# A decoder layer on one core: attention's TensorE work in a written order, projections as counted steps between its parts

## The chip, the cores and the metric

One core of a Trainium2 chip runs the whole kernel. Its engines are TensorE (matrix products, PE in the profile, with its weight loads as PEld), VectorE (DVE), ScalarE (ACT), GpSimd (POOL) and SyncE (SP), which here only issues loads. TensorE reads SBUF and writes PSUM, which has eight banks of 128 x 512 numbers. The metric is device time in microseconds, the median of three runs.

## The reference, cut to what matters

One layer of a hybrid decoder, 512 tokens of width 1024, all in float32. A combined projection of the input gives queries, keys and values of 16 heads of 64, forget gates, the inputs of a state-space branch, and two gates.

```python
q, k, v, f_logit, z, xbc, dt_raw, gate_logit = jnp.split(x @ w_in, ...)
# attention, per head, causal: logit[t, s] = q_t.k_s / 8 + sum of log f between s and t
p = jax.nn.softmax(jnp.where(causal, s, -jnp.inf), axis=-1)
attn = p @ v
gates = sigmoid(gate_logit + b_gates)           # two gates of width 1024
mixed = (gates[0] * (attn @ w_pa) + gates[1] * (ssm @ w_ps)) @ w_out
x = layer_norm(ALPHA * x + mixed)
x = layer_norm(ALPHA * x + (silu(x @ w_fg) * (x @ w_fu)) @ w_fd)
```

## The kernel before

Every float32 operand of a large product is split into a high part (a cast to a shorter format, on ScalarE) and a low part (the difference, on VectorE): `split`, L102 and L103. A product is then three matrix instructions, high by high, high by low and low by high (`mm3`, L144 to L146), which add up in one PSUM bank. There are two kinds of banks, four each: `gps` for projections, `cps` for everything else.

Weights are loaded by SP in chunks of 512 KB (`raw`, four buffers) and split into `whi` and `wlo` (three buffers each, L102 and L103, with priority). A projection is either weight-stationary (`gemm_ws`, 256 output columns into two banks; with the 1024 inputs it is 16 steps of `mm3`, 48 instructions of 512 columns, from two chunks) or input-stationary (`gemm_xs`, 512 output columns into four banks, 32 steps, 96 instructions, four chunks).

The order of the stages is: the state-space branch in four groups, then attention (around L676 of the listing), the second gate `g1` (L690 on), the first gate `g0`, the output projections, the feed-forward part. Each engine works through its queue in order. That order is fixed when the program is built: a scheduler takes instructions by their place in the program text (those under `high_priority` earlier) as their inputs come ready by its own estimate of times. Where a block stands under `manual_schedule`, the engines named in it keep the order of the program text.

Attention works in four groups of four heads. Per group, `att_qk` projects queries and keys (one `gemm_ws` each) and lays them out per head in two tiles: one of 64 rows of the high part with four rows of gate sums under it, which GpSimd fills (L424 memset, L426 and L428 row copies), and one of 128 rows. Their evacuation is a copy on ScalarE (L429), a cast (L430) and a subtraction (L431) on VectorE per head. `att_v` projects the values of two groups at once (`gemm_xs`, L444 and L445). Then `att_head`, for each head:

- scores: for each of four blocks of 128 queries one `cps` bank and two products of 128 to 512 columns (L458, L459);
- softmax per block: mask, negated maximum (L463, VectorE), exponential with row sum (L465, ScalarE), reciprocal (L466) and scaling (L467) on VectorE, in a probability tile `t_y`, of which there are four;
- ten transposes of 128 x 128 into three `cps` banks (L480), each bank split into high and low;
- eight value products into one `cps` bank (L486), of which both halves are added (ScalarE copies one, L490, VectorE adds, L491). Every second head the result is split into `oT`.

The second gate takes a tanh from a `gps` bank into a `t_y` tile (L694) and multiplies `sd`, the state-space result, with it (L695). In the text, projections of a group stand ahead of its heads and the second gate behind all of them; what stands where on TensorE is the scheduler's choice.

Of the kernel before, what the change touches and what calls it, by code (L numbers as in the profile page):

```python
# [2 lines left out]

# [10 lines left out]
ALU = mybir.AluOpType  # L14
# [27 lines left out]
def tile_hybrid_decoder_layer(  # L42
# [62 lines left out]
    def gps():  # L105
        return psum.tile([P, T], F32, name="gps", bufs=4)
# [44 lines left out]
    def gemm_ws(w, c0, nk, rhs, evac, alloc=gps, n=T, chunks=None):  # L151
# [9 lines left out]
        for b in range(2):  # L161
            evac(b, ps[b])

    def gemm_xs(w, c0, lhs, evac, before=None):


        ps = [gps() for _ in range(NT)]
# [11 lines left out]
        if before is None:  # L179
            for kc in range(KD // 2):  # L180
                hi, lo = split_w(fetch(kc), T)
                for tt in range(NT):
                    product(kc, tt, hi, lo)
            return
# [5 lines left out]
        with tc.manual_schedule(engines=ORDERED):  # L190
            for i in range(NT):
# [6 lines left out]
                for tt in range(i + 1):  # L198
                    product(i, tt, *chunks[i])

# [212 lines left out]
    def att_qk(hg, isq, qk):  # L413
        c0 = (C_Q if isq else C_K) + hg * 256
# [19 lines left out]
        gemm_ws(w_in, c0, KD, rhs_x, evac)  # L434

    def att_v(hg):
# [9 lines left out]
        gemm_xs(w_in, C_V + hg * 256, lhs_x, evac)  # L446
        return vt

    def att_head(h, qk, vt, of):
        hh = h % 4  # L450
# [3 lines left out]
        for i in range(NT):  # L454
# [13 lines left out]
            pr.append(pt)  # L468
        ab = big("uh" if h % 2 == 0 else "ul", 4, F32R)
        cc = slot("sq" if h % 2 == 0 else "xw", (P, 2, 256), F32R)  # L470
        pT = {}
        for j, kbs in enumerate(((0,), (1, 3), (2,))):
# [9 lines left out]
            split(hi[:, 0:o], lo[:, 0:o], ps[:, 0:o])  # L482
        po = cps()
# [180 lines left out]
    att_qk(0, True, qk)  # L664
    att_qk(0, False, qk)
# [9 lines left out]
    for hg in range(4):  # L675
        if hg > 0:  # L676
            att_qk(hg, True, qk)
            att_qk(hg, False, qk)
        if hg % 2 == 0:
            vts = att_v(hg)  # L680
        vt = vts[hg % 2]
        for h in range(4 * hg, 4 * hg + 4):
            if h % 2 == 0:
                of = slot("dx")
            att_head(h, qk, vt, of)
            if h % 2 == 1:
                split(oT[h // 2][0], oT[h // 2][1], of)


    for pair in range(4):  # L690
        def evac_g1(b, ps):
            j = 2 * pair + b
# [3 lines left out]
        gemm_ws(w_in, C_G + D + pair * 256, KD, rhs_x, evac_g1)  # L696
# [398 lines left out]
```

## Time and profile before

| | us |
|---|---|
| median of three runs | 1146.16 (1146.07 to 1146.4) |
| the profiled execution's own time | 1149.0 |
| its span, first to last instruction | 1147.3 |
| value projection of heads 0 to 7 | 438.00 to 459.76 |
| first score to last value product | 459.76 to 641.96 |
| rest of the second gate | 641.96 to 661.08 |

A row's start is given in us from the first instruction of the span. The end of a matrix instruction is modelled, and successive ones overlap, so two starts next to each other tell the pace, not the printed duration. Idle time is printed only where nothing at all is under way on the engine by that model.

### The profile page before, as it was taken

Reading aid. Unit: us, or ns where it says so; the run is one execution under the profiler, and the core shown is the slowest. Engines: PE = TensorE matmul, PEld = TensorE weight load, DVE = VectorE, ACT = ScalarE, POOL = GpSimd, SP = SyncE. Lnnn points to the kernel's source line nnn. Section 1 sums busy time; section 2 is a strip of 40 time slices with the busy share of each in tenths; the row PEclk is TensorE's granted clock in tenths of the full one; section 3 lists DMA queues with packets and bytes.
Section 4 is the critical chain, followed back from the end, with each engine's and each line's share of the span. In section 5 each row is a group of like instructions: output and inputs, shape, how many; then the busy total and the mean of one; then the engine's idle time right before and its main releaser. Section 6 shows DMA issues by size and latency. Waiting matters only on the chain.

```text
span 1147.3 us, 15795 instructions
## 1 busy us (share of the span) xinstructions
PE 1118.0 (97%) x6086; PEld 941.3 (82%) x6086; DVE 777.8 (68%) x1223; ACT 527.2 (46%) x912; POOL 134.1 (12%) x165
## 2 busy tenths in 40 slices
PE   7999999999999999999999999999999999999996
PEld 5887778778787788777777888888999999988885
DVE  2679974884786563889598534556997777767326
ACT  2476664454542432666465434214654554453210
POOL 3003130030122100221110000011111111100001
PEclk9999999999999999999999999999999999999998
DMA  6353233233232233211212245381778787465311
GB/s 195 110 169 127 75 112 101 82 111 101 83 94 58 89 92 96 70 57 56 77 53 56 76 127 183 108 204 59 199 184 204 183 195 164 91 231 174 102 55 74
DMA packets 116060, 134.20 MB, mean 117 GB/s; under 512 B 5669, under 2 KB 94481, under 8 KB 115857
## 3 DMA queue, kind: packets, MB, share of 16 engines
q1 hardware_dynamic: 98896, 111.75, 31.8%
q0 software_dynamic: 14640, 14.10, 7.7%
q10 hardware_dynamic: 2448, 7.34, 1.8%
q8 instruction: 48, 0.79, 0.3%
q14 instruction: 28, 0.22, 0.1%
HBM read 128.78 MB, written 4.26 MB: 116 GB/s over the span
## 4 chain that ended last, share of the span: by engine, by line
PE 44%; DVE 3%; issue 3%; DMA 2%; ACT 1%; POOL 0%; POOLq 0%; DVEq 0%; ACTq 0%
PE gps L145 9%; PE gps L144 9%; PE gps L146 9%; PE cps L145 5%; PE cps L146 5%; PE cps L144 4%; DMA rq<-in_w_ffn_up_dram 1%; PE cps L480 1%; PE cps L486 1%; DMA t_sd<-in_x_dram 0%; DVE xr L763 0%; PE cps L458 0%; DMA raw<-in_w_ffn_down_dram 0%; PE cps L459 0%; DVE wlo L103 0%
## 5 line engine op out<-in xcount | busy, mean ns | idle before, releaser
L103 DVE TENSOR_TENSOR wlo<-raw,whi 128x1024 fp32r<-128x1024 f32 x127 | 156.2, 1230 | 189.3 <-ACT whi L102 188.6
L102 ACT CAST whi<-raw 128x1024 fp32r<-128x1024 f32 x127 | 133.4, 1051 | 253.5 <-PE gps L145 101.9
L145 PE MATMUL gps<-xl,whi 128*128 128x512 f32 x456 | 181.2, 397 | 0.0
L144 PE MATMUL gps<-xh,whi 128*128 128x512 f32 x456 | 181.0, 397 | 0.0
L146 PE MATMUL gps<-xh,wlo 128*128 128x512 f32 x456 | 180.8, 396 | 0.0
L102 ACT CAST wh<-rq 128x1024 fp32r<-128x1024 f32 (+1 forms) x84 | 82.2, 980 | 101.7 <-PE cps L145 44.6
L103 DVE TENSOR_TENSOR wl<-rq,wh 128x1024 fp32r<-128x1024 f32 (+1 forms) x84 | 95.0, 1132 | 34.2 <-ACT wh L102 34.1
L144 PEld LDWEIGHTS gps<-xh,whi 128*128 128x128 f32 x456 | 85.9, 188 | 16.3 <-issue 0.2
L145 PEld LDWEIGHTS gps<-xl,whi 128*128 128x128 f32 x456 | 86.0, 189 | 16.1 <-issue 0.2
L146 PEld LDWEIGHTS gps<-xh,wlo 128*128 128x128 f32 x456 | 86.0, 189 | 15.4
L144 PE MATMUL gps<-whi,xh 128*128 128x512 f32 x192 | 76.1, 397 | 1.9 <-ACT whi L102 1.6
L145 PE MATMUL gps<-wlo,xh 128*128 128x512 f32 x192 | 75.8, 395 | 1.0 <-DVE wlo L103 1.0
L146 PE MATMUL gps<-whi,xl 128*128 128x512 f32 x192 | 75.8, 395 | 0.0
L265 DVE SCALAR_TENSOR_TENSOR t_v<-gps,cw,t_v 128x511 f32<-128x511 f32 (+2 forms) x72 | 53.4, 745 | 3.9 <-ACT t_v L262 3.1
L145 PE MATMUL gps<-t_ul,whi 128*128 128x512 f32 x128 | 51.1, 399 | 0.0
L146 PE MATMUL gps<-t_uh,wlo 128*128 128x512 f32 x128 | 51.0, 399 | 0.0
L144 PE MATMUL gps<-t_uh,whi 128*128 128x512 f32 x128 | 50.5, 394 | 0.0
L144 PEld LDWEIGHTS gps<-whi,xh 128*128 128x128 f32 x192 | 36.5, 190 | 10.7 <-ACT whi L102 2.0
L465 ACT ACTIVATE t_y<-t_y,sm 128x128 f32<-128x128 f32 (+1 forms) x64 | 35.7, 559 | 19.4 <-DVE sm L463 17.7
L347 ACT ACTIVATE t_ab<-t_ab,acum 128x128 f32<-128x128 f32 x128 | 41.6, 391 | 5.7 <-DMA t_ab<-ac_d 5.4
L821 POOL DMA_DIRECT2D rq<-in_w_ffn_gate_dram x12 | 15.5, 1294 | 245.7 <-ACT xh L723 159.0
L145 PEld LDWEIGHTS gps<-wlo,xh 128*128 128x128 f32 x192 | 36.5, 190 | 9.3 <-DVE wlo L103 1.9
(567 smaller groups left out, 2761.3 us busy)
## 6 DMA issues: line engine op xcount, KB each, us to landing
raw<-in_w_in_dram SPq DMA_DIRECT2D x80, 512.0 KB, 3.7
rq<-in_w_ffn_gate_dram SPq DMA_DIRECT2D x25, 512.0 KB, 5.8
rq<-in_w_ffn_up_dram SPq DMA_DIRECT2D x25, 512.0 KB, 5.9
raw<-in_w_ffn_down_dram SPq DMA_DIRECT2D x22, 512.0 KB, 4.0
t_ab<-ac_d SPq DMA_DIRECT2D x32, 256.0 KB, 3.3
raw<-in_w_proj_ssm_dram SPq DMA_DIRECT2D x16, 512.0 KB, 3.5
rq<-in_w_ffn_gate_dram POOLq DMA_DIRECT2D x10, 512.0 KB, 7.8
rq<-in_w_ffn_up_dram POOLq DMA_DIRECT2D x10, 512.0 KB, 6.4
```

The source lines that it names most:

```text
L102: nc.scalar.copy(out=hi, in_=src)
L103: nc.vector.tensor_tensor(out=lo, in0=src, in1=hi.bitcast(F32), op=ALU.subtract)
L144: nc.tensor.matmul(out=o, lhsT=l[0], rhs=r[0], start=start, stop=False, skip_group_check=skip)
L145: nc.tensor.matmul(out=o, lhsT=l[0], rhs=r[1], start=False, stop=False, skip_group_check=skip)
L146: nc.tensor.matmul(out=o, lhsT=l[1], rhs=r[0], start=False, stop=stop, skip_group_check=skip)
L265: nc.vector.scalar_tensor_tensor(out=v[:, sh:], in0=ps[:, 0:T - sh], scalar=cw[:, k, blk:blk + 1], in1=v[:, sh:], op0=ALU.mult, op1=ALU.add)
L347: nc.scalar.activation(out=m[:, r, :], in_=m[:, r, :], func=AF.Relu, scale=-1.0, bias=acum[:, c, h:h + 1])
L465: nc.scalar.activation(out=pt[:, 0:n], in_=pt[:, 0:n], func=AF.Exp, scale=-1.0, bias=sm[:, 2:3], accum_out=sm[:, 0:1])
L480: nc.tensor.transpose(out=ps[:, o:o + P], in_=pr[i][:, kb * P:(kb + 1) * P], identity=ident)
L486: nc.tensor.matmul(out=po[:, kb * P:], lhsT=vt[:, kb, hh, :], rhs=pT[kb][j], start=kb == 0 and j == 0, stop=kb == NT - 1 and j == 1)
L821: nc.gpsimd.dma_start(out=self.v(t), in_=self.q(*s_), accum_op=ALU.add)
```

## The change

`gemm_ws` and the plain form of `gemm_xs` become generators (`ws_steps`, `xs_steps`) that issue one step of three products at each call, and evacuate a bank as soon as its last step is issued. `att_head` is cut in three: `att_scores` with the softmax, `att_transposes`, `att_values`. The whole attention part stands under `manual_schedule` for TensorE, so there the text is the order: scores of the next head, a number of steps (`before_t`, 7 if not listed), values of the head before, ten transposes, a number of steps (`after_t`, 3), and so on. The steps come in a chain: queries and keys of group 1, a quarter of the second gate, queries and keys of group 2 (80 steps, heads 0 to 7), then values of groups 2 and 3, queries and keys of group 3, the rest of the second gate (112 steps). On the other engines, scores with softmax, and transposes with their splits, stand under `high_priority`. The second gate's tanh is written into its own bank, not into a `t_y` tile.

```diff
-        for b in range(2):
-            evac(b, ps[b])
+                    if half == nk // 4 - 1 and k == 3:
+                        evac(b, ps[b])
+                    yield
...
+    def xs_steps(w, c0, lhs, evac):
+        ps = [gps() for _ in range(NT)]
+        for kc in range(KD // 2):
+            hi, lo = load_w(w[kc * 256:(kc + 1) * 256, c0:c0 + T], 2, T)
+            for tt in range(NT):
+                for k in range(2):
+                    kt = kc * 2 + k
+                    mm3(ps[tt], lhs(kt, tt), (hi[k], lo[k]), kt == 0, kt == KD - 1)
+                    if kt == KD - 1:
+                        evac(tt, ps[tt])
+                    yield
...
-    for hg in range(4):
-        if hg > 0:
-            att_qk(hg, True, qk)
-            att_qk(hg, False, qk)
-        if hg % 2 == 0:
-            vts = att_v(hg)
-        vt = vts[hg % 2]
-        for h in range(4 * hg, 4 * hg + 4):
...
-            att_head(h, qk, vt, of)
...
-            th = slot("y")
-            nc.scalar.activation(out=th, in_=ps, func=AF.Tanh, scale=0.5, bias=vec[:, 32 + j:33 + j])
-            nc.vector.scalar_tensor_tensor(out=sd[j], in0=th, scalar=1.0, in1=sd[j], op0=ALU.add, op1=ALU.mult)
+                nc.scalar.activation(out=ps, in_=ps, func=AF.Tanh, scale=0.5, bias=vec[:, 32 + j:33 + j])
+                nc.vector.scalar_tensor_tensor(out=sd[j], in0=ps, scalar=1.0, in1=sd[j], op0=ALU.add, op1=ALU.mult)
+            yield from ws_steps(w_in, C_G + D + pair * 256, KD, rhs_x, evac_g1)
+    with tc.manual_schedule(engines={mybir.EngineType.PE}):
+        vts, steps = att_v(0)
...
+        def finish(h, pT):
...
+            att_values(h, pT, vts[(h // 4) % 2], of[0])
...
+        pr, pT = att_scores(0, qk), None
+        gates = gates1()
+        steps = chain(*(att_qk(1, isq, qk) for isq in (True, False)), islice(gates, 16), *(att_qk(2, isq, qk) for isq in (True, False)))
+        before_t = {8: 10, 9: 12, 10: 10, 11: 14, 12: 6, 13: 6, 14: 6}
+        after_t = {8: 4, 9: 4, 10: 4, 11: 8, 12: 3, 13: 4, 14: 3}
+        for h in range(AH):
+            fill(before_t.get(h, 7))
+            if pT is not None:
+                finish(h - 1, pT)
+            with tc.high_priority():
+                pT = att_transposes(h, pr)
+            fill(after_t.get(h, 3))
+            if h == 7:
+                finish(h, pT)
+                pT = None
+                vts, steps = att_v(2)
+                steps = chain(steps, *(att_qk(3, isq, qk) for isq in (True, False)), gates)
+                fill(8)
+            if h < AH - 1:
+                with tc.high_priority():
+                    pr = att_scores(h + 1, qk)
+        finish(AH - 1, pT)
```

How the order on the engines moves is shown at two places. The first is TensorE in the first heads. Before, from the third group of transposes of head 0 (`cps<-ident,t_y`) to its first value products (`cps<-t_uh,t_xtok`); `gps<-xh,whi` and its like are products of a projection:

```order
L480 MATMUL cps<-ident,t_y 128x128 x3
L145 MATMUL gps<-xl_98,whi 128x512
L146 MATMUL gps<-xh_96,wlo 128x512
L144 MATMUL gps<-xh_96,whi 128x512
L145 MATMUL gps<-xl_98,whi 128x512
L480 MATMUL cps<-ident,t_y 128x128 x4
L146 MATMUL gps<-xh_96,wlo 128x512
L144 MATMUL gps<-xh_96,whi 128x512
L486 MATMUL cps<-t_uh,t_xtok 128x512
L145 MATMUL gps<-xl_98,whi 128x512
L146 MATMUL gps<-xh_96,wlo 128x512
L486 MATMUL cps<-t_uh,t_xtok 128x512
```

Now, from the last step ahead of head 0's value products to the first step behind head 1's transposes (the lines count differently in the changed file: L145 to L147 are `mm3`, L499 the transposes, L509 the value products):

```order
L145 MATMUL gps<-xh_96,whi 128x512
L146 MATMUL gps<-xl_98,whi 128x512
L147 MATMUL gps<-xh_96,wlo 128x512
L509 MATMUL cps<-t_uh,t_xtok 128x512 x2
L509 MATMUL cps<-t_uh,t_xtok 128x384 x2
L509 MATMUL cps<-t_sq,t_xtok 128x256 x2
L509 MATMUL cps<-t_uh,t_xtok 128x128 x2
L499 MATMUL cps<-ident,t_y 128x128 x10
L145 MATMUL gps<-xh_96,whi 128x512
L146 MATMUL gps<-xl_98,whi 128x512
L147 MATMUL gps<-xh_96,wlo 128x512
```

Transposes came in groups of one to four, and value products one by one, with products of a projection between them; now eight value products and ten transposes stand in one piece.

The second place is VectorE between the softmax of one head and the next. Before, from the last scaled tile of head 2 (`t_y<-t_y,sm`) over the splits of its transposes (`t_uh`, `t_sq`) and the first masked scores of head 3 (`t_y,sm<-cps,mneg`) to the sum of head 2's values (`t_dx<-cps,t_yo`):

```order
L467 TENSOR_SCALAR t_y<-t_y,sm 128x512
L431 SCALAR_TENSOR_TENSOR t_cbm<-gps,t_btok 64x512
L103 TENSOR_TENSOR t_uh<-cps,t_uh 128x512 x2
L103 TENSOR_TENSOR t_sq<-cps,t_sq 128x256
L463 ISA t_y,sm<-cps,mneg 128x128
L463 ISA sm 128x1
L463 ISA t_y,sm<-cps,mneg 128x256
L463 ISA sm 128x1
L466 RECIPROCAL sm<-sm 128x1
L463 ISA t_y,sm<-cps,mneg 128x384
L463 ISA sm 128x1
L491 TENSOR_TENSOR t_dx<-cps,t_yo 64x512
```

Now, from the last scaled tile of head 2 over the sum of head 1's values and the splits of head 2's transposes to the masked scores of head 3 (L479 masks, L483 scales, L514 sums, L104 splits, `wlo` is a weight chunk's low part):

```order
L483 TENSOR_SCALAR t_y<-t_y,sm 128x512
L104 TENSOR_TENSOR wlo<-raw,whi 128x1024
L514 TENSOR_TENSOR t_dx<-cps,t_yo 64x512
L104 TENSOR_TENSOR t_uh<-cps,t_uh 128x512 x2
L104 TENSOR_TENSOR t_sq<-cps,t_sq 128x256
L104 TENSOR_TENSOR t_hn<-t_dx,t_hn 128x512
L448 CAST t_th<-t_v 64x512
L479 ISA t_y,sm<-cps,mneg 128x128
L479 ISA sm 128x1
L479 ISA t_y,sm<-cps,mneg 128x256
```

The sum of a head's values stood among the masked scores of the next head; now the sum of the head before, and the splits, come behind the softmax and a weight split, and ahead of the next head's masked scores.

## Rows read from the trace of the kernel before

**Rows 1.** Page, busy time of each engine: us (share of the span) xinstructions

```profile
PE 1118.0 (97%) x6086; PEld 941.3 (82%) x6086; DVE 777.8 (68%) x1223; ACT 527.2 (46%) x912; POOL 134.1 (12%) x165
```

**Rows 2.** Windows: from:to us, busy (xcount) PE PEld DVE ACT POOL, clock, DMA

```profile
438.00:459.76 21.76, 21.76 (x98) 18.02 (x96) 7.44 (x10) 6.03 (x10) 0.00 (x0) 1.00 0.32 94
459.76:641.96 182.20, 180.79 (x910) 140.47 (x908) 151.31 (x410) 113.09 (x258) 24.83 (x48) 1.00 0.22 61
641.96:661.08 19.12, 19.12 (x87) 15.82 (x86) 7.04 (x8) 6.36 (x9) 0.00 (x0) 1.00 0.34 100
```

**Rows 3.** Timeline of PE: start, us, engine line op out<-in xcount [idle<-releaser]

```profile
438.00 0.39 PE L144 MATMUL gps<-whi,xh 128*128 128x512 f32 x1
...
459.76 0.22 PE L458 MATMUL cps<-t_v,t_btok 68*128 68x128 f32 x1
...
461.05 0.40 PE L144 MATMUL gps<-xh,whi 128*128 128x512 f32 x1
...
661.08 0.39 PE L144 MATMUL gps<-xh,whi 128*128 128x512 f32 x1
```

**Rows 4.** Groups of PE, 459.76 to 641.9: xcount | busy us, mean ns

```profile
L144 PE MATMUL gps<-xh,whi 128*128 128x512 f32 x132 | 53.7, 407 | 0.0
...
L144 PE MATMUL gps<-whi,xh 128*128 128x512 f32 x32 | 12.6, 394 | 0.0
```

**Rows 5.** Timeline of PE: four transposes, one product, and the next product's start

```profile
475.28 0.60 PE L480 MATMUL cps<-ident,t_y 128*128 128x128 f32 x4
...
475.95 0.40 PE L145 MATMUL gps<-xl,whi 128*128 128x512 f32 x1
```

**Rows 6.** Timeline of PE: value products of 256 and 128 columns in head 1

```profile
477.87 0.28 PE L486 MATMUL cps<-t_xw,t_xtok 128*128 128x256 f32 x1
477.99 0.22 PE L459 MATMUL cps<-t_th,t_cbm 128*128 128x128 f32 x1
...
478.22 0.33 PE L486 MATMUL cps<-t_ul,t_xtok 128*128 128x128 f32 x2
478.39 0.33 PE L458 MATMUL cps<-t_v,t_btok 68*128 68x256 f32 x1
```

**Rows 7.** Waits, 459.76 to 641.9: who waited for whom: us, times, longest us

```profile
PEld cps L480 <- DVE t_y L467: 11.4, 37, 0.8
...
PEld cps L458 <- DVE sm L463: 2.3, 5, 0.6
```

**Rows 8.** Timeline of PE: a score behind a product

```profile
470.20 0.40 PE L144 MATMUL gps<-xh,whi 128*128 128x512 f32 x1
470.81 0.50 PE L458 MATMUL cps<-t_bT,t_xst 68*128 68x512 f32 x1 [0.22 <-DVE sm L463]
```

**Rows 9.** Timeline of DVE: the last probability tile of head 0

```profile
465.86 0.49 DVE L467 TENSOR_SCALAR t_y<-t_y,sm 128x512 f32<-128x512 f32 x1
```

**Rows 10.** Timelines of ACT, then DVE: transposes' splits, values' copy and sum

```profile
475.59 1.07 ACT L102 CAST t_ul<-cps 128x512 fp32r<-128x512 f32 x2 [0.55 <-PE cps L480]
...
478.64 0.58 ACT L490 COPY t_yo<-cps 64x512 f32<-64x512 f32 x1 [1.08 <-PE cps L486]
...
476.24 1.29 DVE L103 TENSOR_TENSOR t_ul<-cps,t_ul 128x512 fp32r<-128x512 f32 x2
...
479.60 0.68 DVE L491 TENSOR_TENSOR t_dx<-cps,t_yo 64x512 f32<-64x512 f32 x1
```

**Rows 11.** Groups of DVE, 459.76 to 641.9: the fill's own work

```profile
L103 DVE TENSOR_TENSOR wlo<-raw,whi 128x1024 fp32r<-128x1024 f32 x21 | 25.7, 1224 | 12.9 <-ACT whi L102 12.7
...
L445 DVE TENSOR_TENSOR t_xtok<-gps,t_xtok 128x256 fp32r<-128x256 f32 x11 | 4.5, 421 | 1.8 <-ACT t_xtok L444 1.8
...
L431 DVE SCALAR_TENSOR_TENSOR t_xdt<-gps,t_xst 64x512 fp32r<-64x512 f32 x6 | 4.2, 695 | 0.1
...
L695 DVE SCALAR_TENSOR_TENSOR t_sd<-t_y,t_sd 128x512 f32<-128x512 f32 x4 | 2.6, 683 | 0.0
...
L430 DVE CAST t_th<-t_v 64x512 fp32r<-64x512 f32 x6 | 2.6, 427 | 0.2
```

More of the change, by code (lines that the diff above doesn't have):

```diff
@@ L2 @@
 from contextlib import ExitStack
+from itertools import chain, islice
 import concourse.bass as bass
@@ L160, in gemm_ws @@
                     mm3(ps[b], (hi[k][:, bs], lo[k][:, bs]), rhs(kt), kt == 0, kt == nk - 1)
-        for b in range(2):
-            evac(b, ps[b])
+                    if half == nk // 4 - 1 and k == 3:
+                        evac(b, ps[b])
+                    yield
     def gemm_xs(w, c0, lhs, evac, before=None):
-        ps = [gps() for _ in range(NT)]
+        ps = [] if before is None else [gps() for _ in range(NT)]
         def fetch(kc):
@@ L179, in gemm_xs @@
         if before is None:
[L180 to L183, printed above, removed]
+            for _ in xs_steps(w, c0, lhs, evac):
+                pass
             return
@@ L482, in att_head, with att_values @@
             split(hi[:, 0:o], lo[:, 0:o], ps[:, 0:o])
+        return pT
+    def att_values(h, pT, vt, of):
+        hh = h % 4
         po = cps()
@@ L663, in tile_hybrid_decoder_layer @@
                 group_x(g + 1, st, pair)
-    att_qk(0, True, qk)
-    att_qk(0, False, qk)
+    for isq in (True, False):
+        for _ in att_qk(0, isq, qk):
+            pass
     group_proj(NG - 1, u)
@@ L674, in tile_hybrid_decoder_layer, with gates1, evac_g1 @@
     oT = [(oslots[2 * i], oslots[2 * i + 1]) for i in range(KD)]
[L675 to L682 removed]
+    def gates1():
+        for pair in range(4):
+            def evac_g1(b, ps, pair=pair):
+                j = 2 * pair + b
+                nc.scalar.activation(out=ps, in_=ps, func=AF.Tanh, scale=0.5, bias=vec[:, 32 + j:33 + j])
+                nc.vector.scalar_tensor_tensor(out=sd[j], in0=ps, scalar=1.0, in1=sd[j], op0=ALU.add, op1=ALU.mult)
+            yield from ws_steps(w_in, C_G + D + pair * 256, KD, rhs_x, evac_g1)
@@ L683, in tile_hybrid_decoder_layer, with fill @@
+    with tc.manual_schedule(engines={mybir.EngineType.PE}):
+        vts, steps = att_v(0)
+        for _ in steps:
+            pass
+        of = {}
+        def finish(h, pT):
             if h % 2 == 0:
-                of = slot("dx")
-            att_head(h, qk, vt, of)
+                of[0] = slot("dx")
+            att_values(h, pT, vts[(h // 4) % 2], of[0])
             if h % 2 == 1:
[L687 to L692, printed above, removed]
-            th = slot("y")
-            nc.scalar.activation(out=th, in_=ps, func=AF.Tanh, scale=0.5, bias=vec[:, 32 + j:33 + j])
-            nc.vector.scalar_tensor_tensor(out=sd[j], in0=th, scalar=1.0, in1=sd[j], op0=ALU.add, op1=ALU.mult)
-        gemm_ws(w_in, C_G + D + pair * 256, KD, rhs_x, evac_g1)
+                split(oT[h // 2][0], oT[h // 2][1], of[0])
+        def fill(n):
+            for _ in range(n):
+                if next(steps, 0) == 0:
+                    break
+        pr, pT = att_scores(0, qk), None
[20 more added lines that the diff above has]
+        finish(AH - 1, pT)
+        for _ in steps:
+            pass
```

15 lines of the change are left out of this document (9 added, 6 removed).

## The prediction

> **What bounds the kernel now.** The page's first view comes first: TensorE is busy for 97% of the span [rows 1], so the kernel can only get shorter where TensorE gets its products out faster. The busy share does not say where that is. The view by windows splits the part that the change touches into three stretches [rows 2]: the value projection ahead of head 0 (438.00 to 459.76 us), the 16 attention heads (459.76 to 641.96), and the rest of the second gate's projections (641.96 to 661.08). TensorE shows as busy in all three (99% in the middle), at a granted clock of 1.00. VectorE is at 34%, 83% and 37%.
>
> The timeline gives the pace. The value projection is 96 products of 512 columns, from the first at 438.00 to the first score at 459.76 [rows 3]: 21.76 / 96 = 0.2267 us a product. The middle stretch has 3 x 132 + 3 x 32 = 492 such products [rows 4], and the tail 576 - 492 = 84 (19.12 / 84 = 0.228, full pace again). Three prices for attention's own work, each read where the instructions stand together:
> - scores of one head, 8 products: 459.76 to 461.05, 1.29 us [rows 3];
> - transposes: four of them and one 512-column product take 475.28 to 475.95, so (0.67 - 0.23) / 4 = 0.11 each, 1.11 for ten [rows 5];
> - value products, 8 a head: two of 512 columns at 0.227, two of 384 at 0.17 (between the 512 and the 256), two of 256 at 0.12 and the last two together 0.17 [rows 6], 1.20 in all.
>
> A head costs 3.60, sixteen 57.6. So the middle stretch would take 492 x 0.2267 + 57.6 = 169.1 at those prices, and it takes 182.2: 13.1 us are lost there, inside time that the profile calls busy. The list of waits shows how: the weight loads wait 11.4 us in 37 places for a scaled probability tile ahead of a transpose, and 2.3 us in 5 places for a score's bank [rows 7]. In the timeline one blocked score stands 0.61 us behind the product before it, of which only 0.22 are printed as idle [rows 8].
>
> Here a rule and the first view disagree. By TensorE's busy time the middle stretch has 182.20 - 180.79 = 1.4 us to give [rows 2]. The Trainium skill (Perfetto Trace Analysis, Identifying the Most-Contended Engine) calls matmul busy time a poor measure, since the instructions are pipelined, and looks at the share of weight loads instead. This trace sides with it: weight loads are busy 83% at full pace and 77% among the heads [rows 2]. Scaled by that ratio the stretch would lose about 13 us, as an estimate. The sum below uses the starts alone.
>
> **The change part by part.** (1) The order. Before, a transpose, a value product or a score stands between two products of a projection wherever the scheduler put it, and TensorE stops there if its input is late. Now each head is: scores, 7 steps of a projection (a step is 3 products, 0.68 us), the value products of the head before, ten transposes, 3 steps, the next scores. No product is added or removed: 576 of 512 columns and 16 heads stand in both, from the first score to the first product of the next gate. Before, that takes 661.08 - 459.76 = 201.3 us [rows 3]. Without a single wait it would now take 576 x 0.2267 + 57.6 = 188.2. The ceiling of the gain is 13.1.
>
> (2) What is late next. I follow one steady head from the start of its scores, at 0. Scores end at 1.29, the 7 steps at 6.05, the value products at 7.25, the transposes at 8.36, the 3 steps at 10.4. The transposes need all four probability tiles. In head 0 of before, with a weight split and a value tile of the projection queued among them on VectorE, the last tile is scaled at 465.86 + 0.49 = 466.35 [rows 9], 6.6 after the first score; so in a steady head they are there with 0.7 or more to spare. Only in head 0, which has no value products in front, does the fourth transpose come early: 461.05 + 21 x 0.2267 + 0.33 = 466.14, a wait of about 0.3, with the restart 0.4.
> The tight place is the next scores at 10.4, each of which needs one of four score banks. These are freed by the value product's copy and sum (0.58 on ScalarE, 0.68 on VectorE) and by the three splits of the transposes (two copies in 1.07, two subtractions in 1.29, a third of half the width) [rows 10]. The value products end at 7.25, their sum at about 7.25 + 0.25 + 0.58 + 0.68 = 8.8, and the subtractions follow at 9.4, 10.0 and 10.4, while the four scores start at 10.4, 10.6, 10.9 and 11.2. It fits with 0.4 to 0.8 to spare if VectorE has nothing else queued ahead.
>
> (3) VectorE's share. Its work does not change: 151.3 + 7.0 us in the two stretches [rows 2], 84% of 188.2. It is only placed otherwise. Per projection of queries or keys the fill costs VectorE two weight splits, four casts and four subtractions, 2 x 1.22 + 4 x 0.41 + 4 x 0.69 = 6.9; per pair of gate columns 2 x 1.22 + 2 x 0.68 = 3.8 [rows 11]. The first 80 steps, spread over heads 0 to 7, are four of the former and one of the latter, 31.4 in all. The groups of fill in the middle stretch add to 25.7 + 4.5 + 16.6 + 2.6 + 9.9 = 59.3 (the third and the last are four groups each, of which one stands in the rows). A head's own work lies then between (151.3 - 59.3) / 16 = 5.75, and (182.2 - 59.3) / 16 = 7.7 if VectorE had no idle at all there. Heads 0 to 7 thus need 77 to 93 us of VectorE and 80 x 0.68 + 8 x 3.60 = 83.2 of TensorE. I take the low end, since it is the measured busy time, and the upper one takes all idle for work. Heads 8 to 15 have 112 steps: 105.0 of TensorE, and of VectorE 33.4 for the fill and 46 to 62 for the heads, always less. The one crowded head is head 3, where nine casts and subtractions and two weight splits fall together, 14 us of full durations; VectorE has caught up by head 4, whose own queue holds one weight split and one subtraction.
>
> (4) The gate's tanh now stays in its bank, and the sum reads it there. That frees the four probability buffers for heads alone, and holds a projection bank for one VectorE instruction longer. No row shows a tanh written to a bank; by the nearest, the same instruction into SBUF and the subtractions that read a bank (0.68 to 0.69 [rows 11]), it is from -0.3 to +0.3 us for each of 8. All eight lie beside TensorE's work, with two free banks: 0 on the path; if that cover were gone, 2.4. (5) The evacuation of a projection's first half is written earlier, which moves nothing that TensorE waits for; outside this part the order on the engines is as before. (6) SP's queue keeps its order of loads, and POOL's its memsets and row copies.
>
> Costs left over: 0.4 in head 0, and at the seams of 16 heads (three changes between kinds of products, a bank that is just late) between 0 and 0.6 a head. The low end is a seam as at 461.05, which costs 0.01 to 0.02, the high end is the blocked score of before. I take 0.15, near the low end, as the bank has 0.4 to spare: 2.4. So 13.1 - 0.4 - 2.4 = 10.3, and I forecast 10: the profiled span goes from 1147.3 to 1137.3, its execution from 1149.0 to 1139.0, and the median of the runs, which lies 2.8 under that execution, from 1146.16 to 1136.2.
>
> **The rivals.**
> - VectorE paces heads 0 to 7. For it: it is 83% busy in the middle stretch, and head 3 has 14 us of it against 10.4 of TensorE. Against: that 83% comes with the same work. At the upper bound it costs 92.8 - 83.2 = 9.6: 188.2 + 9.6 = 197.8, and the median is 1142.7; halfway 1138 to 1140.
> - The scores wait for their banks in every head, and the kernel gets slower. TensorE can no longer run a projection past a late score, and only 2 us of fill stand between the transposes and the scores. For it: before already has scores that wait for a bank [rows 7, 8], and in the order a weight split (1.22) stands on VectorE ahead of the value sum and the splits. If that split starts late, sum and splits end up to 1.2 later, and the scores wait up to 0.8. From 13.1 / 16 = 0.82 a head on, the gain is eaten. With the split and a half-evacuated projection (1.1 more) ahead, it is 1.9 - 0.8 = about 1 a head more: 1147 to 1150. Against: the weight split is released long before the value products end, so VectorE is through with it by then. The Trainium skill (Perfetto Trace Analysis, Optimization Strategy) reads the same gap coming back as a sign of too few buffers for the next tile; four banks for four scores, three transposes and one sum are that case, and the printed waits of before agree in kind.
> - Nothing moves. TensorE is as full as it can be, as its busy row says, and the gaps between starts are the price of changing between kinds of products. Then at most 1.4 come back, 1144.8 to 1146.2. For it: a lone transpose among products costs more than 0.11. Against: the 13.7 us for which the weight loads wait [rows 7] have names of late tiles.
>
> **How the numbers follow.** The forecast, TensorE at its pace with small seams, has 0.70 and lies between 1133.2 (no wait at all) and 1139.5. VectorE as the pace has 0.16 (1138 to 1143), nothing moves 0.08, the banks 0.06. A difference of 0.2% (2.3 us) is about what a measurement of this kernel tells from none: faster 0.86, same 0.08, slower 0.06. The range for 8 in 10 is 1133.0 to 1143.0.
>
> **What would show it.** In the profile after: from the first score to the first product of the next gate 189 to 194 us, where 201.3 were; heads 1, 2, 4 and 5 at 10.4 to 10.7 from score to score; the weight loads' wait for scaled tiles under 2 us; VectorE's busy time over the stretch as before, near 158. The forecast is wrong if that stretch is over 195: with waits of transposes for scaled tiles in heads 2 to 7 it is VectorE, with waits of scores for the splits of the transposes it is the banks. If the stretch is shorter by 10 and the span is not, the time was given back in the next gate or the FFN, which I hold for unlikely, since TensorE bounds those too.

## The result, and the profile after

The changed kernel takes 1137.33 us (median of four runs, 1135.88 to 1138.17) against 1146.28 of the kernel before: a ratio of 0.9914, 95% interval 0.9902 to 0.9926. Run again beside other runs of the kernel before, it took 1137.15 (0.9918, 0.9904 to 0.9933). The forecast was 1136.2 in a range of 1133.0 to 1143.0.

The view by windows, as in [rows 2]: the value projection ahead of head 0, then what is called the stage from here on, from the first score to the first product of the next gate (the last two rows of [rows 2] together).

```profile
438.72:460.48 21.76, 21.76 (x98) 18.02 (x97) 7.43 (x10) 6.03 (x10) 0.00 (x0) 1.00 0.33 94
460.48:651.85 191.37, 190.83 (x994) 163.16 (x992) 157.20 (x417) 118.83 (x266) 25.04 (x48) 1.00 0.24 68
```

The value projection takes the same 21.76. The stage takes 191.37 instead of 201.32 [rows 3], so 9.95 of the gain is there. VectorE does the same work in it, 157.2 against 151.3 + 7.0. The share of weight loads, by which the prediction judged the loss, went from (140.47 + 15.82) / 201.32 = 78% to 85%. It shows the direction and not the size: it is now above the 83% of the value projection while 3.2 us are still lost, and about as many weight loads (992, before 994) show as 163.2 us where they showed as 156.3. That the prediction's scaling by 83% came to the same 13 us was luck. The page's PE row barely moved, from 97% to 98%:

```profile
PE 1108.9 (98%) x6086; PEld 947.4 (83%) x6086; DVE 777.3 (68%) x1223; ACT 526.4 (46%) x912; POOL 134.2 (12%) x165
```

The list of waits of the weight loads in the stage, which answers to [rows 7]:

```profile
PEld cps L509 <- DVE t_xtok L463: 0.5, 1, 0.5
PEld cps L474 <- DVE t_ul L104: 0.5, 2, 0.3
PEld cps L499 <- DVE t_y L483: 0.3, 1, 0.3
...
```

(The two rows left out, 0.3 us each, have no releaser.) Transposes waited 11.4 us in 37 places for a scaled tile; now it is 0.3 in one. Two rows of the list of before, which the prediction passes over, are gone as well: value products that wait for the splits of the transposes. With the two rows of the subtractions (1.1 and 1.0) they come to 7.1 us.

```profile
PEld cps L486 <- ACT t_uh L102: 2.5, 8, 0.3
PEld cps L486 <- ACT t_ul L102: 2.5, 7, 0.6
```

A weight load that waits can still overlap the product before it, so these times are not a sum of what TensorE lost: with the 13.7 us that the prediction names they make 20.8, where the starts give 13.1. The timeline of TensorE in the changed kernel, at the end of head 1, shows a whole pass without a wait (L145 to L147 are the projections, L474 and L475 the scores, L499 the transposes, L509 the value products):

```profile
476.08 0.96 PE L509 MATMUL cps<-t_uh,t_xtok 128*128 128x512 f32 x4
...
477.29 1.28 PE L499 MATMUL cps<-ident,t_y 128*128 128x128 f32 x10
478.32 0.48 PE L145 MATMUL gps<-xh,whi 128*128 128x512 f32 x1
478.64 0.40 PE L146 MATMUL gps<-xl,whi 128*128 128x512 f32 x1
...
480.50 0.23 PE L474 MATMUL cps<-t_v,t_btok 68*128 68x128 f32 x1
...
481.79 0.40 PE L145 MATMUL gps<-xh,whi 128*128 128x512 f32 x1
```

Value products take 1.21 (1.20 foreseen), scores 1.29 (1.29), ten transposes and the product behind them 1.35 (1.11 + 0.23 = 1.34 foreseen). From first score to first score the heads take, by the starts in the timeline:

| head | 0 | 1 | 2 | 3 | 4 | 5 | 6 | 9 | 10 |
|---|---|---|---|---|---|---|---|---|---|
| us | 9.55 | 10.48 | 10.47 | 10.47 | 11.09 | 10.47 | 10.47 | 15.17 | 13.20 |
| at full pace | 9.20 | 10.40 | 10.40 | 10.40 | 10.40 | 10.40 | 10.40 | 14.48 | 13.12 |

(Head 0 has no value products; heads 9 and 10 have 16 and 14 steps. Of the heads not shown, 7 and 13 are 0.3 over full pace.) An undisturbed head is 0.07 to 0.08 over. The three that stand out are head 0, whose fourth transpose waits for its tile, head 4, whose scores wait for their banks (t_ul is a split that frees one), and head 9, whose value products wait for VectorE to finish the value projection's last tile. The waits above have these three names. For head 9, TensorE's row and then the one of VectorE for which it waits:

```profile
573.03 0.40 PE L509 MATMUL cps<-t_sq,t_xtok 128*128 128x256 f32 x2
573.77 0.44 PE L509 MATMUL cps<-t_uh,t_xtok 128*128 128x128 f32 x2 [0.34 <-DVE t_xtok L463]
```

```profile
572.15 1.23 DVE L104 TENSOR_TENSOR wlo<-raw,whi 128x1024 fp32r<-128x1024 f32 x1 [0.76 <-ACT whi L103]
573.30 0.42 DVE L463 TENSOR_TENSOR t_xtok<-gps,t_xtok 128x256 fp32r<-128x256 f32 x1
```

A weight split of 1.23 us stands ahead of the last part of the value tile, which is done at 573.72.

### The profile page after: what moved, and what is told of

The parts are those of the page before. It is cut to its first block, busy times and chain, and to the rows that moved or that the text cites. A ratio compares the mean times of both kernels' runs of the same rounds, so it can differ in the third digit from the quotient of the medians.

```text
span 1136.5 us, 15815 instructions
## 1 busy us (share of the span) xinstructions
PE 1108.9 (98%) x6086; PEld 947.4 (83%) x6086; DVE 777.3 (68%) x1223; ACT 526.4 (46%) x912; POOL 134.2 (12%) x165
## 4 chain that ended last, share of the span: by engine, by line
PE 81%; DVE 9%; issue 4%; POOL 2%; DMA 2%; ACT 2%; POOLq 0%; DVEq 0%; ACTq 0%
PE gps L147 19%; PE gps L146 19%; PE gps L145 19%; PE cps L146 5%; PE cps L147 5%; PE cps L145 5%; PE cps L509 2%; DVE wlo L104 1%; PE cps L499 1%; PE cps L370 1%; DMA rq<-in_w_ffn_up_dram 1%; ACT whi L103 1%; PE cps L474 1%; PE cps L475 1%; PE cps L328 1%
## 5 line engine op out<-in xcount | busy, mean ns | idle before, releaser
L104 DVE TENSOR_TENSOR wlo<-raw,whi 128x1024 fp32r<-128x1024 f32 x127 | 156.2, 1230 | 177.5 <-ACT whi L103 176.5
L145 PE MATMUL gps<-xh,whi 128*128 128x512 f32 x456 | 180.8, 396 | 0.0
L147 PE MATMUL gps<-xh,wlo 128*128 128x512 f32 x456 | 179.6, 394 | 0.0
L104 DVE TENSOR_TENSOR wl<-rq,wh 128x1024 fp32r<-128x1024 f32 (+1 forms) x84 | 94.8, 1130 | 33.2 <-ACT wh L103 33.1
L145 PEld LDWEIGHTS gps<-xh,whi 128*128 128x128 f32 x456 | 86.0, 189 | 17.4 <-issue 0.2
L147 PEld LDWEIGHTS gps<-xh,wlo 128*128 128x128 f32 x456 | 85.9, 188 | 17.5
L145 PE MATMUL gps<-whi,xh 128*128 128x512 f32 x192 | 76.3, 397 | 1.9 <-ACT whi L103 1.6
L147 PE MATMUL gps<-whi,xl 128*128 128x512 f32 x192 | 75.5, 393 | 0.0
L147 PE MATMUL gps<-t_uh,wlo 128*128 128x512 f32 x128 | 51.0, 399 | 0.0
L145 PE MATMUL gps<-t_uh,whi 128*128 128x512 f32 x128 | 50.5, 395 | 0.0
L145 PEld LDWEIGHTS gps<-whi,xh 128*128 128x128 f32 x192 | 36.4, 190 | 10.4 <-ACT whi L103 2.0
L147 PEld LDWEIGHTS gps<-whi,xl 128*128 128x128 f32 x192 | 36.4, 190 | 8.6 <-DVE xl L104 1.1
```

What stands on the lines that cost most here:

```text
L104: nc.vector.tensor_tensor(out=lo, in0=src, in1=hi.bitcast(F32), op=ALU.subtract)
L145: nc.tensor.matmul(out=o, lhsT=l[0], rhs=r[0], start=start, stop=False, skip_group_check=skip)
L147: nc.tensor.matmul(out=o, lhsT=l[1], rhs=r[0], start=False, stop=stop, skip_group_check=skip)
```

## The experiments

Three theories were to be told apart. A: TensorE's order of before put transposes, scores and value products where their inputs were late, and the written order gives the gain. B: the priority on the other engines gives it. C: the time was the price of changing between kinds of products. All runs and what came of them; "stage" is as above, read from the starts in each profile, and each ratio is to the kernel before, run beside it.

| kernel | median us | ratio to before, 95% interval | stage us |
|---|---|---|---|
| before | 1146.28 | 1 | 201.32 |
| after | 1137.33 | 0.9914, 0.9902 to 0.9926 | 191.37 |
| old_order_priority | 1155.68 | 1.0084, 1.0069 to 1.0099 | 210.58 |
| old_order_control | 1162.68 | 1.0134, 1.0114 to 1.0154 | 216.86 |
| no_priority | 1142.35 | 0.9967, 0.9956 to 0.9977 | 196.06 |
| mixed_transposes | 1141.00 | 0.9950, 0.9935 to 0.9965 | 194.68 |
| old_spread_of_fill | 1140.81 | 0.9952, 0.9938 to 0.9967 | 195.57 |
| transposes_2us_earlier | 1141.53 | 0.9948, 0.9931 to 0.9964 | 195.61 |
| scores_1.4us_earlier | 1143.30 | 0.9963, 0.9952 to 0.9975 | 197.3 |
| tanh_in_a_tile | 1135.31 | 0.9898, 0.9883 to 0.9912 | 191.08 |
| after_again | 1137.15 | 0.9918, 0.9904 to 0.9933 | 191.39 |
| gaps_closed | 1135.89 | 0.9905, 0.9888 to 0.9921 | 190.64 |
| gaps_closed_tanh_in_a_tile | 1136.58 | 0.9915, 0.9899 to 0.9930 | 190.39 |

### The old order, with priority and without

The attention part was written so that TensorE goes through the same kinds and shapes of products in the same order as in the kernel before, by a list of counts (S a score, P a projection product, T a transpose, V a value product; code shortened).

```diff
+ORDER = "S8 P12 T P T2 P3 T3 P4 T4 P2 V P2 V2 S V2 S V3 S4 P S2 P6 T P T2 P4 T3 ..."
...
+        for kind, n in ORDER:
+            for _ in range(n):
+                next(work[kind])     # S, and T with its splits, under high_priority
```

> TensorE keeps, product for product, the order of the kernel before (transposes, value products and scores strewn among the projections), but the scores' chain and the transposes with their splits have priority on the other engines, as after, and the tanh stays in its bank. All work is done. Stage from the first score to the first product of the next gate: 201.3 us before, 191.4 after. Theory A (TensorE's written order gives the gain, since the order of before puts products where their inputs are late): 198 to 202, time 1143 to 1147. Theory B (the priority on VectorE and ScalarE gives it, and TensorE's order is nearly free): 191 to 194, time 1137 to 1140. Theory C (the loss of before is the price of changing between kinds of products): unchanged, 201, time 1146; A and C are told apart by mixed_transposes.

Measured: 210.58 and 1155.68, so slower than before, where no theory had put it. So the priority, with the old order of TensorE, does not give the gain that B said. A's number missed too, and the trace says why. The timelines of VectorE in head 1, first of before (L463 negated maximum, L467 scaling), then of this kernel (L500, L504):

```profile
472.36 0.55 DVE L467 TENSOR_SCALAR t_y<-t_y,sm 128x128 f32<-128x128 f32 x2
472.81 0.68 DVE L463 CUSTOM_DVE_ANT_0 t_y<-cps,mneg 128x512 f32<-128x512 f32 x1
...
474.65 0.48 DVE L467 TENSOR_SCALAR t_y<-t_y,sm 128x512 f32<-128x512 f32 x1
```

```profile
471.72 0.69 DVE L500 CUSTOM_DVE_ANT_0 t_y<-cps,mneg 128x512 f32<-128x512 f32 x1
...
473.13 0.26 DVE L504 TENSOR_SCALAR t_y<-t_y,sm 128x128 f32<-128x128 f32 x1
...
473.38 1.06 DVE L504 TENSOR_SCALAR t_y<-t_y,sm 128x256 f32<-128x256 f32 x3
```

With priority, the last tile is ready earlier (474.44 against 475.13) and the first later (473.39 against 472.6), as all four maxima now run ahead of the first scaling. But the old order wants the first tile first. TensorE, before and in this kernel (here L526 is a transpose, L164 a product of the projection):

```profile
472.76 0.27 PE L480 MATMUL cps<-ident,t_y 128*128 128x128 f32 x1
```

```profile
473.45 0.33 PE L526 MATMUL cps<-ident,t_y 128*128 128x128 f32 x1 [0.38 <-DVE t_y L504]
473.53 0.48 PE L164 MATMUL gps<-xl,whi 128*128 128x512 f32 x1
```

The products behind the late transpose come in their order, so most heads keep what their first transpose loses. Measured from each head's first score, the first transposes of the sixteen heads come later than before by 9.1 us in all; the stage is 9.3 longer. (Head by head it is rougher: heads 3 and 11 get theirs back, and behind head 7 a projection waits 1.4 us for its bank.) The Trainium skill (PSUM — Partial Sum Buffer, Engine vs sequencer instructions) says that products on TensorE start in program order, though a weight load may go ahead; the rows agree, since the projection product waits with the transpose.

The same kernel without the priorities was the control.

```diff
-                    with tc.high_priority():
-                        next(work[kind])
+                    next(work[kind])
```

> The kernel of old_order_priority without the priorities: TensorE in the order of the kernel before, the other engines ordered by the scheduler. That one took 210.6 us in the stage and 1155.7 us, 9 over before, with its first probability tile of a head 0.5 to 1 us later and its last 0.6 to 1.3 earlier than before. If the priority is what made it slower (it reorders VectorE for tiles that TensorE's order does not want first): back to 200 to 203, time 1145 to 1148. If the fixed order of TensorE as such, or the other way of writing the code, cost it: 208 to 211, time 1153 to 1156.

Measured: 216.86 and 1162.68, slower still, and both expectations missed. Part of the 216.86 is the clock: in the profiled execution a stretch at a lower granted clock (0.60 in the row below, the column ahead of the last two) falls into head 11, which takes 16.29 us where head 3, whose order on TensorE is the same, takes 15.04 (in before the two take 11.81 and 11.82). In no other profile does one fall into the stage.

```profile
606.00:608.00 2.00, 2.00 (x9) 1.52 (x8) 0.00 (x0) 0.25 (x1) 0.00 (x0) 0.60 0.82 252
```

Less these 1.25, the stage is about 215.6. So the priority was not the harm; it is worth about 5 us of the stage here, and the kernel before does about 14 better with the same order on TensorE. Between them the order on the other engines differs, the tanh's place, and the point at which the second value tiles are taken. This kernel's largest wait in the stage (L525 is a transpose):

```profile
PEld cps L525 <- DVE t_y L504: 18.8, 33, 3.0
...
```

In before it was 11.4 with at most 0.8 at once [rows 7]. In head 3 the trace shows what VectorE's order does. Its second tile is scaled at 491.27 in before, 3.8 us after the head's first score, and here at 494.95, 6.7 us after it, behind a cast and a subtraction of the fill, the last negated maximum and a weight split; TensorE stands for it. The rows of VectorE in before and here, and the one of TensorE here:

```profile
491.27 0.34 DVE L467 TENSOR_SCALAR t_y<-t_y,sm 128x256 f32<-128x256 f32 x1
```

```profile
494.95 0.67 DVE L504 TENSOR_SCALAR t_y<-t_y,sm 128x256 f32<-128x256 f32 x2
```

```profile
495.35 0.44 PE L525 MATMUL cps<-ident,t_y 128*128 128x128 f32 x2 [2.52 <-DVE t_y L504]
```

So the old order of TensorE takes from 201 to about 216 us, as VectorE's order fits it or not; that the scheduler had made both together in the kernel before is the likely reason for its fit, and stays an argument.

### The written order without priority

```diff
-                with tc.high_priority():
-                    pr = att_scores(h + 1, qk)
+                pr = att_scores(h + 1, qk)
```

(The transposes likewise.)

> After without the two priorities; TensorE's order is that of after, word for word. Theory A: casts and subtractions of the fill then stand on VectorE ahead of probabilities and splits, by up to 1 to 3 us, of which heads 1, 2 and 5 have 2 to 3 to spare and heads 3, 4 and 7 nothing: stage 193 to 197 instead of 191.4, time 1139 to 1143. Theory B: the stage goes back to about 201, time 1146 to 1147. Theory C: unchanged, 191.4, time 1137.

Measured: 196.06 and 1142.35, within A. Nearly all of the 4.7 comes from few heads, above all head 3 (12.96 instead of 10.47):

```profile
497.98 0.84 PE L499 MATMUL cps<-ident,t_y 128*128 128x128 f32 x3
500.79 0.98 PE L499 MATMUL cps<-ident,t_y 128*128 128x128 f32 x7 [1.96 <-DVE t_y L483]
```

```profile
498.47 0.42 DVE L448 CAST t_th<-t_v 64x512 fp32r<-64x512 f32 x1
498.90 0.68 DVE L449 SCALAR_TENSOR_TENSOR t_th<-gps,t_v 64x512 fp32r<-64x512 f32 x1
...
499.65 0.68 DVE L514 TENSOR_TENSOR t_dx<-cps,t_yo 64x512 f32<-64x512 f32 x1
500.26 0.47 DVE L483 TENSOR_SCALAR t_y<-t_y,sm 128x512 f32<-128x512 f32 x1
```

A cast and a subtraction of the fill, and a value sum, stand ahead of the scaling for which TensorE waits. So with the written order the priority is worth 4.7 and with the old one about 5; the written order is worth 19.5 without the priority and 19.2 with it, against the old order written by hand, and 5.3 and 10.0 against the kernel before.

### Lone transposes among products

```diff
+                    if not (kb == 2 and i == NT - 1):
+                        between()                       # one product of a projection
...
-            fill(before_t.get(h, 7))
+            fill(before_t.get(h, 7) - (0 if h == 9 else 2))
```

> After, but each head's ten transposes alternate with nine single products of the projection (two steps of the fill ahead of them and one behind are used for that), so that TensorE changes between kinds 350 to 370 times in the stage, where before changes 259 times and after about 80. All work is done. Theory C, the 13.1 us lost before being the price of such changes (0.07 us each): stage 208 to 213 instead of 191.4, time 1154 to 1159. Theories A and B: a lone transpose with its input ready costs no more than one among others; only heads 0, 3 and 4, whose last probabilities come 6.6, 7.4 and 7.6 us after the first score, wait 0.5 to 0.9 each: stage 191 to 195, time 1137 to 1141.

Measured: 194.68 and 1141.00, within A and far from C. In head 2, where the tiles are early:

```profile
487.25 0.27 PE L506 MATMUL cps<-ident,t_y 128*128 128x128 f32 x1
487.27 0.48 PE L151 MATMUL gps<-xl,whi 128*128 128x512 f32 x1
487.59 0.27 PE L506 MATMUL cps<-ident,t_y 128*128 128x128 f32 x1
...
490.01 0.27 PE L506 MATMUL cps<-ident,t_y 128*128 128x128 f32 x1
```

Eight pairs of a transpose and a product take 490.01 - 487.25 = 2.76, 0.345 a pair; less 0.2267 that is 0.118 for a lone transpose, beside 0.11 in a block. Head 2 takes 10.54 instead of 10.47. Changing between transposes and products costs next to nothing, and C falls; lone value products and scores were not tried by themselves. The rest of the 3.3 is transposes that wait for tiles (L506) and scores that wait for a bank (L480 in this kernel), in heads 0, 1, 5 and 7, where heads 0, 3 and 4 were expected:

```profile
PEld cps L480 <- DVE t_sq L104: 1.8, 3, 0.7
PEld cps L506 <- DVE t_y L489: 1.4, 3, 1.0
```

### The fill spread as before

```diff
-        before_t = {8: 10, 9: 12, 10: 10, 11: 14, 12: 6, 13: 6, 14: 6}
+        before_t = {12: 7, 13: 7, 14: 7, 15: 7}
...
-            fill(before_t.get(h, 7))
+            fill(before_t.get(h, 5))
...
-                fill(8)
+                fill(32)
```

> TensorE in a written order with the priorities, but the projections are spread as before: 8 steps a head in heads 0 to 6 and 8 to 11 (5 ahead of the value products, 3 behind the transposes), the value projection of 32 steps in one piece behind head 7, the gate's in heads 12 to 15 and behind. All work is done. A head with 8 steps is 8 x 0.68 + 3.6 = 9.0 us of TensorE, and VectorE has 5.75 to 7.7 of its own work in it and 3.5 of fill. If the spread matters (VectorE paces such heads, and is idle in the 32 steps): 0.3 to 1.2 us a head in 11 or 12 heads, stage 195 to 203, time 1141 to 1149. If it doesn't: 191 to 193, time 1137 to 1139.

Measured: 195.57 and 1140.81, at the low end of the first case (the time 0.2 under it). Waits for scaled tiles are nearly the only ones:

```profile
PEld cps L499 <- DVE t_y L483: 6.0, 11, 1.1
```

With 8 steps, the fourth transpose stands 6.3 us behind the first score, and the last tiles come at 6.2 to 6.9 in most heads, so they take 9.3 to 9.9 us instead of 9.04. Over heads 2 to 5 (476.87 to 514.81) VectorE is busy 36.42 of 37.94 us, 96%. This is the rival of the prediction in which VectorE paces the heads; it comes at 8 steps a head, and the 10 steps of the change avoid it.

### Transposes earlier, scores earlier

```diff
-            fill(before_t.get(h, 7))
+            fill(before_t.get(h, 7) - (0 if h == 9 else 3))
...
-            fill(after_t.get(h, 3))
+            fill(after_t.get(h, 3) + (0 if h == 9 else 3))
```

> After with three steps of the fill moved from ahead of the value products to behind the transposes in every head but head 9: the transposes come 2.04 us earlier, the fourth at 5.6 instead of 7.6 us after the first score. By the times at which after has the last probability tile (6.6, 7.4, 7.6 and 6.4 us in heads 0, 3, 4 and 7, at most 5.7 in the others), the theory of late tiles gives waits of 2.2, 1.8, 2.0 and 0.8 us and 0 to 0.2 elsewhere, less 0.4 that head 0 waits already and 0.6 of the score banks of head 4: stage 195 to 199 instead of 191.4, time 1141 to 1145. If the place of the transposes does not matter: 191, time 1137.

Measured: 195.61 and 1141.53, within the expectation, but spread otherwise: heads 0 and 7 lose 2.0 and 1.8, head 3 loses 1.3, and head 4, for which 2.0 less 0.6 was expected, gains 0.5, since VectorE's order moved too and its last tile comes at 5.6 instead of 7.6.

```diff
-            fill(before_t.get(h, 7))
+            fill(before_t.get(h, 7) + 2)
...
-            fill(after_t.get(h, 3))
+            fill(after_t.get(h, 3) - 2)
```

> After with two steps of the fill moved from behind the transposes to ahead of the value products in every head: one step, 0.68 us, is left between the transposes and the next scores, so that value products and transposes end 1.36 us later against the next scores. By the working of the prediction the value sum then frees its bank 10.2 us into the head and the splits free theirs at 10.7, 11.3 and 11.7, where scores are wanted at 10.4, 10.6, 10.9 and 11.2: 0.4 to 0.8 us a head in 13 to 15 heads. Theory of the four score banks: stage 197 to 203, time 1143 to 1149. If banks are no limit: 190 to 192, time 1136 to 1138.

Measured: 197.3 and 1143.30, both within the expectation. The stage needs care here, because three products of the next gate stand ahead of the last value products, and the first product behind them starts at 657.72: 657.72 - 459.75 - 3 x 0.2267 = 197.3. (The 577th product, by which the other stages end, starts at 655.76, ahead of the last head's value products.)

```profile
655.76 0.39 PE L147 MATMUL gps<-xh,wlo 128*128 128x512 f32 x1
...
657.55 0.33 PE L509 MATMUL cps<-t_ul,t_xtok 128*128 128x128 f32 x2
657.72 0.45 PE L145 MATMUL gps<-xh,whi 128*128 128x512 f32 x1
```

The wait is the one named:

```profile
PEld cps L474 <- DVE t_uh L104: 4.4, 12, 1.1
PEld cps L474 <- DVE t_ul L104: 1.5, 6, 0.3
```

Heads 1 to 6 take 11.06 to 11.85, and head 7 takes 1.4 more than in after; of the later ones, whose VectorE has less to do, only heads 13 and 15 lose 0.6. So four score banks are a limit, and the two steps more that the change leaves behind the transposes are enough to keep off it, in all heads but head 4, and by 0.2 head 13.

### The tanh's place, and the gaps left over

```diff
-                nc.scalar.activation(out=ps, in_=ps, func=AF.Tanh, ...)
+                th = slot("y")
+                nc.scalar.activation(out=th, in_=ps, func=AF.Tanh, ...)
```

> After with the gate's tanh written to one of the probability tiles, as before, instead of to its bank. By the prediction's working, nothing on the path: stage 190.5 to 192.5, time 1136 to 1139. If the tile taken from the heads' four matters, a head among the eight that meet a gate's half waits for its tile until the gate's sum is through, 0.7 us or more for each: stage 194 to 198, time 1140 to 1144.

> The changed kernel once more, as the yardstick for the two versions run beside it: stage 191.4, time 1136 to 1138.

```diff
-        before_t = {8: 10, 9: 12, 10: 10, 11: 14, 12: 6, 13: 6, 14: 6}
-        after_t = {8: 4, 9: 4, 10: 4, 11: 8, 12: 3, 13: 4, 14: 3}
+        before_t = {0: 8, 5: 6, 6: 6, 8: 10, 9: 14, 10: 8, 11: 14, 12: 6, 13: 6, 14: 6}
+        after_t = {3: 4, 8: 4, 9: 4, 10: 4, 11: 8, 12: 3, 13: 4, 14: 3}
```

> After with four steps of the fill shifted at the places where it still waits: one more ahead of the transposes of head 0 (0.36 us there) and one more ahead of the scores of head 4 (0.6), taken from heads 5 and 6 whose last tiles are early; two more ahead of the value products in head 9 (0.6, they wait for the value projection's evacuation), taken from head 10. Theory of late inputs: 1.2 to 1.6 us less, stage 189.5 to 190.5, time 1.0 to 2.0 under after_again. If the waits only move on to the next head: stage 191 to 192, time as after_again.

> gaps_closed with the tanh in a probability tile as in tanh_in_a_tile, whose time was 2.0 us under the changed kernel's on another chip at a stage only 0.3 shorter. If the tile is worth nothing, stage and time are those of gaps_closed within 0.5; if it is worth the 2 us of those runs, the time is 1.5 to 2.5 under gaps_closed.

With the tanh in a tile the stage is 191.08, as foreseen. The time, 1135.31, came out under the expectation and 2.0 under the changed kernel's; beside gaps_closed the same edit is 0.7 slower (1136.58 against 1135.89). So the tanh's place is worth nothing that these runs can tell. By the groups of the stage (the changed kernel, then the tile) the instruction itself is cheaper into the bank, a mean of 660 ns against 707 over eight, off the path.

Closing the gaps gave 0.75 of the stage where 1.2 to 1.6 was expected. The waits in heads 0, 4 and 9 are gone, as meant, but head 11 takes 0.6 more, since its last score waits for the bank of the value sum:

```profile
PE cps L474 <- DVE t_dx L514: 0.4, 1, 0.4
```

Its 1135.89 against 1137.15 of the changed kernel run beside it is less than the runs can tell apart (the intervals of the ratios overlap). It beats the kernel before; whether it beats the changed one is open.

## Why the prediction was right

**The place and the ceiling.** The working said that 13.1 us of the stage were lost to late inputs and that the written order takes them away. The stage fell by 9.95 (10.3 foreseen), with a head at 10.47 (10.4 to 10.7 foreseen, for heads 1, 2 and 5; head 4 missed it with 11.09), the waits for scaled tiles at 0.3 (under 2), and VectorE's work at 157.2 (158). The price of changing kinds, the "nothing moves" rival, was tried by itself and is 0.008 us a transpose.

**What is left over.** Foreseen were 0.4 in head 0 and 2.4 at seams, 2.8 in all; it is 191.37 - 188.2 = 3.2. The sum was nearly right, its terms were not. Head 0 loses 0.35. The seams are 0.07 to 0.08 a head instead of the 0.15 taken, 1.2 in all. The other 1.6 is heads 4 (0.6) and 9 (0.6), and 0.2 each in heads 7 and 13. For head 0 the working wrote a wait of about 0.3; its own times give 466.35 - 466.14 = 0.2. Head 9's wait, for the evacuation of a value projection that the change pulled close to its first use, is a step that the working did not have.

**Head 3 and the banks.** The working gave the last tile at 6.6 us into a steady head, 0.7 ahead of the transposes, and had VectorE caught up by head 4. In head 3 that tile is ready at 497.87 + 0.47 = 498.34, 7.37 into the head, and in head 4 at 7.61; the fourth transpose of a steady head stands at 7.62. So the transposes just fit; the crowd lasted one head longer than stated, and head 4's scores paid for it. The working gave each score 0.4 to 0.8 to spare. Its own times (banks free at 8.8, 9.4, 10.0 and 10.4, scores at 10.4, 10.6, 10.9 and 11.2) give 0.8 to 1.6, and head 2 is like that, with value sum and subtractions through at 8.8, 9.5, 10.1 and 10.5 us into the head. In head 3 the sum ends at 10.2, 1.35 later, and the subtractions with it, which is more than there was to spare. The row of head 3's last tile, then head 4's scores; the third score comes 0.60 behind the second, where it is 0.29 in head 2 (480.67 to 480.96):

```profile
497.87 0.47 DVE L483 TENSOR_SCALAR t_y<-t_y,sm 128x512 f32<-128x512 f32 x1
```

```profile
501.79 0.39 PE L474 MATMUL cps<-t_v,t_btok 68*128 68x256 f32 x1
502.02 0.28 PE L475 MATMUL cps<-t_th,t_cbm 128*128 128x256 f32 x1
502.39 0.45 PE L474 MATMUL cps<-t_v,t_btok 68*128 68x384 f32 x1
```

Both rivals were thus real and near: VectorE paces the heads at 8 steps (old_spread_of_fill), and the banks hold up the scores with one step behind the transposes (scores_1.4us_earlier). Neither made the kernel slower than before, at 4 to 6 us of the stage each. The price that the prediction put on the banks, 1147 to 1150, does not follow from its working: about 1 us more in each of 16 heads would be 1162.

**From the span to the median.** The profiled execution was forecast at 1139.0 and took 1138.17. The median was put 2.8 under it, the distance in the kernel before; here it is 0.84. That term was mis-sized: it belongs to one execution, not to the kernel. Outside the stage the profiles of the thirteen kernels above take from 942.7 to 946.4 us, with 945.9 for before, near the upper end. So the medians fell by 9.0 and 9.3, against the forecast of 10.

**The parts of the change.** The prediction put all of the gain on the order. By the runs, half stands without the priority (201.3 to 196.1) and the other half with it (to 191.4), and the spread of the fill is worth 4.2. The weakest statement is the one behind it, that the loss sits in TensorE's order alone: with that order and another on VectorE it is 13 to 27 us, so the loss of before belongs to the pair of orders. The working followed VectorE through a head without a word on the priority, and without it head 3's last tile comes at 10.0 instead of 7.4. No run tries the earlier evacuation of a projection's first half by itself; it is in every version here but before.

## What to carry to other kernels

Small dependent products strewn among large ones on an in-order engine each have a slack of their own, and the first late one shifts the rest; gathered in one block, behind counted independent work that lasts until the worst head's last input is there, they share one. It is the counted work that does it more than the block: mixed_transposes strews the transposes again, behind five counted steps, and loses 3.3 us. Check the other side as well: the work behind the block has to outlast the freeing of the banks, and a producer with priority should hand over first what is wanted first. Where the gain is under 1%, compare the changed stretch from start to start in the traces, since single executions here differ by 3.7 us outside of it; and see that the stretch holds the same work at the same clock in both.

## What the runs showed of the hardware

A lone 128 x 128 transpose between two 512-column products costs 0.118 us, against 0.11 in a block.

In the two profiles first compared, one stretch of a low granted clock falls at different places. Windows of the kernel before, then of after:

```profile
810.00:812.00 2.00, 1.91 (x9) 1.91 (x10) 2.00 (x4) 0.41 (x1) 0.07 (x1) 0.58 0.87 207
812.00:814.00 2.00, 2.00 (x13) 2.00 (x12) 2.00 (x3) 0.00 (x0) 0.00 (x0) 0.57 1.18 188
```

```profile
62.00:64.00 2.00, 2.00 (x7) 1.32 (x7) 1.56 (x5) 1.30 (x4) 0.00 (x0) 0.55 0.49 188
64.00:66.00 2.00, 2.00 (x10) 1.49 (x9) 0.60 (x2) 0.57 (x1) 0.00 (x0) 0.60 0.82 336
```

The clock (the column ahead of the last two) is at the lower of its two levels, 1.2 instead of 2.4 GHz, for most of these windows. Ahead of it TensorE had been busy 2.41 of 4 us in before (806 to 810), and 2.00 of 2.00 in after (60 to 62); in old_order_control, whose only such stretch lies in the stage (606 to 610), it had been busy 1.77 of 4. So the rows don't show what sets the place. In after the clock is 1.00 from 796 to 816, where it has the feed-forward part's first products, and TensorE comes through them 1.5 us faster; its attention stage in turn starts 0.7 later. The second profile of the same kernel (after_again) has no such stretch at either place. That is a part of the scatter outside the stage, and no effect of the change: the three profiles without one (but for the first and last microseconds) take 942.7 to 944.4 us outside the stage, the two with two of them 946.1 and 946.4.
